# Projecting q, k and v of the second token half transposed, with the rotary exchange by way of DRAM

## The chip, the cores and the metric

The kernel runs on one core of one Trainium2 chip. The metric is the device time of one execution in microseconds (us).

## The reference

One decoder layer over 1024 tokens of width 1024, in float32. The change concerns the softmax attention of the first sub-layer. Of the combined input projection, 512 columns are q (8 heads of 64), 128 are k and 128 are v (2 heads of 64 each):

```python
proj = h @ w_in[l]
aq, ak, av, hq, hf, hi, hg = jnp.split(proj, _SPLITS, axis=-1)
aq = partial_rope(aq.reshape(B, T, ATT_Q_HEADS, ATT_HEAD_DIM))
ak = partial_rope(ak.reshape(B, T, ATT_KV_HEADS, ATT_HEAD_DIM))
...
attn = sliding_window_sink_attention(aq, ak, av, attn_sinks[l])   # window 128, blocks of 128
attn = rmsnorm(attn, attn_out_w[l])
```

`partial_rope` rotates only the first 16 of the 64 dimensions of a head: with x1 and x2 the first and second 8 of them, it gives x1·cos − x2·sin and x2·cos + x1·sin, where the angle depends on the token. The attention output and that of a gated linear recurrence (from hq, hf, hi, hg) go through one output projection; a dense MLP with hidden width 4096 follows.

## The kernel before

The sequence is cut into 8 blocks of 128 tokens (tb 0 to 7) in two halves (0 to 3, 4 to 7). The normed input h is held transposed (model dimension on the partitions, tokens along the row), for each of 8 slices of the model dimension and each half, as a high and a low part (`hhi`, `hlo`); weights are split likewise. `proj3` forms a product as three matmuls per slice, so one projection of 8 slices is 24 matmuls.

Natural layout: for each block, `hhi`/`hlo` of the block are the stationary operand and the weights stream, giving q as 128 tokens by 512 columns (`pq`) and k with v as 128 by 256 (`pk`). ScalarE (ACT) moves these to SBUF (`q`, `kv`), and `rope` rotates in place along the row, on GpSimd (POOL) for most blocks. The projections of the first half are done in an earlier, hand-ordered stage; those of blocks 4 and 5 of q run while the second half's h is being finished.

`attention(tb)` is a generator with three parts. Part one turns q (four transposes to `pqT`, one ACT copy to `qT`) and k (one transpose to `pkT`, one VectorE (DVE) copy to `kT`), forms the scores `sc` against the block itself and the block before it, copies them into `comb` (ACT copies the previous block's half, DVE's masked copies, COPY_PREDICATED, the block's own), takes the row maximum (`mx`), the exponentials (eight on ACT, into `comb`, with sums), and divides. Part two turns the probabilities (`pT`), masks them into `pc` and `pp`, multiplies with v into `oT`, and starts the norm: `sqa`, `sqr`, a transpose `ssp`, `ssc`, two small POOL operations ending in `r_att`, and `dg`. Part three is the matmul `rb` and a multiplication of `q`. A loop of 16 steps calls these parts for block tb at steps tb+4, tb+6 and tb+7, and after them `filler(i)`: for i below 8 the q or the k/v projection of a second-half block with its rope, above that `values(i-8)`, the projection `pv` of the recurrence's values (24 matmuls of 128x512, from weights `whv`). Instructions are not pinned in this stretch: a scheduler chooses the order on each engine, and each engine then runs its list in that order, waiting at whatever is not ready. Loads are issued from the SyncE (SP) queue; `wada` and `whv` in the rows below are weight loads. After the loop come the recurrence's head projections (`phf`, `phq`, `phg`).

All operations are recorded by a helper, so every row of the profile reads L39.

Of the kernel before, what the change touches and what calls it, by code (L numbers as in the profile page):

```python
# [47 lines left out]
def hybrid_layer(ctx: ExitStack, tc: tile.TileContext, I, out, dbg=None):  # L48
# [476 lines left out]
    def htok(tb):  # L525
        sl = slice(tb % 4 * P, tb % 4 * P + P)
        return [(hh[k][tb // 4][0][:, sl], hh[k][tb // 4][1][:, sl]) for k in range(KB) if hh[k][tb // 4]]
# [2 lines left out]
        return [hh[k][th] for k in range(KB)]  # L530

    qn, kvn = [], []
    cosT = cload("cosT", [P, TB, 16], pool=XA)
    sinT = cload("sinT", [P, TB, 16], pool=XA)

    def qproj(tb):
        if tb < 6:
            pq = pq0[tb]
        else:
            pq = mm_ps(f"pq{tb}")  # L540
            proj3(pq, htok(tb), wq)
        q = m_(f"q{tb}")
        ACT.activation(q, pq, AF.Copy, scale=0.125)
        qn.append(q)

    def kvproj(tb):
        if tb < 4:
            pk = pk0[tb]
        else:
            pk = mm_ps(f"pk{tb}")  # L550
            proj3(pk[:, :256], htok(tb), wkv)
        kv = XA.tile([P, 256], F32, tag="kv", bufs=8, name=f"kv{tb}")
        ACT.activation(kv, pk[:, :256], AF.Copy)
        kvn.append(kv)

    def rope(tb, nh, eng=POOL):
        base = qn[tb] if nh == 8 else kvn[tb][:, 0:P]
        v3 = base.rearrange("p (h d) -> p h d", d=64)
        rt = t_(f"rt{tb}_{nh}", (P, 2, 8, 16))
        t1, t2 = rt[:, 0], rt[:, 1]  # L560
        cb = cosT[:, tb:tb + 1, :].broadcast_to([P, nh, 16])
        s0 = sinT[:, tb:tb + 1, 0:8].broadcast_to([P, nh, 8])
        s1 = sinT[:, tb:tb + 1, 8:16].broadcast_to([P, nh, 8])
        eng.tensor_tensor(t1[:, :nh, :], v3[:, :, 0:16], cb, ALU.mult)
        eng.tensor_tensor(t2[:, :nh, 0:8], v3[:, :, 8:16], s0, ALU.mult)
        eng.tensor_tensor(t2[:, :nh, 8:16], v3[:, :, 0:8], s1, ALU.mult)
        eng.tensor_tensor(v3[:, :, 0:16], t1[:, :nh, :], t2[:, :nh, :], ALU.add)


    sinks = cload("sinks", [P, 8], pool=tiny1)  # L570
# [1 line left out]
    mle = cload("mle", [P, P], I32, pool=XA)  # L572
    fle = cload("fle", [P, P], pool=XA)
    attT = [None] * TB
    kTs, vs = {}, {}

    def attention(tb):
        q, kv = qn[tb], kvn[tb]
        pqT = tp_ps(f"pqT{tb}")
        for m in range(4):  # L580
            PE.transpose(pqT[:, m * P:(m + 1) * P], q[:, m * P:(m + 1) * P], ident)
        qT = t_(f"qT{tb}", [P, 4, P])
        ACT.activation(qT, pqT.rearrange("p (m t) -> p m t", m=4), AF.Copy)
        pkT = tp_ps(f"pkT{tb}")
        PE.transpose(pkT[:, :P], kv[:, 0:P], ident)
        kT = XA.tile([P, P], F32, tag="kT", bufs=3, name=f"kT{tb}")
        DVE.tensor_copy(kT, pkT[:, :P])
        kTs[tb] = kT
        aw = q
        a3 = aw.rearrange("p (m t) -> p m t", m=4)  # L590
        c5 = w_(f"comb{tb}", (P, 2, 2, 2, P))
# [49 lines left out]
                DVE.tensor_tensor(pp[:, mp], pT3, pc[:, mp], ALU.subtract)  # L641
        o_ps = tp_ps(f"oT{tb}")
        for g in range(2):
            vsl = slice(128 + 64 * g, 192 + 64 * g)
            og = o_ps[64 * g:64 * g + 64, :].rearrange("p (a x) -> p a x", a=2)
            if tb:
                PE.matmul(og, lhsT=kvn[tb - 1][:, vsl],
                          rhs=pp[:, :, 2 * g:2 * g + 2, :].rearrange("p a m q -> p a (m q)"), start=True, stop=False)
            PE.matmul(og, lhsT=kv[:, vsl], rhs=pc[:, :, 2 * g:2 * g + 2, :].rearrange("p a m q -> p a (m q)"),
                      start=(tb == 0), stop=True)  # L650
        sq = t_(f"sqa{tb}")
        ACT.activation(sq, o_ps, AF.Square)
# [19 lines left out]
            next(att[tb])  # L672

    att = [attention(tb) for tb in range(TB)]
    pq0.append(a_ps("pq4"))
    for kb in range(KB):
        if 0 < kb < KB - 1:
            if kb + 2 < KB:
                DVE.tensor_tensor(xT1[kb + 2], xT1[kb + 2], rbx, ALU.mult)
            first_evac(1, kb + 1, xT1[kb + 1])  # L680
        (qproj if kb < 4 else kvproj)(kb % 4)
        if kb == 0:
            pq0.append(mm_ps("pq5"))
        for tb in (4, 5):
            proj3(pq0[tb], htok(tb)[kb:kb + 1], wq[kb:kb + 1], kb == 0, kb == KB - 1)
    for tb in range(4):
        eng = DVE if tb < 2 else POOL
        rope(tb, 8, eng)
        rope(tb, 2, eng)
    pin(False, ACT, DVE, POOL, PE)  # L690

    def filler(i):
        if i < 8:
            (kvproj if i % 2 else qproj)(4 + i // 2)
            rope(4 + i // 2, 2 if i % 2 else 8)
        else:
            values(i - 8)


    whv = []  # L700
    hv = []
# [1033 lines left out]
def layout(x, c, w_ada, b_ada, pre_w_mix, w_in, attn_sinks, attn_out_w, lb_table,  # L1735
           hg_norm_w, w_out, post_w_mix, pre_w_mlp, w_up, w_down, post_w_mlp):
    A = {}
    f = lambda a: np.ascontiguousarray(a)
    cols = lambda v: f(np.asarray(v).reshape(-1, P).T)
    A["x"] = f(np.asarray(x)[0])  # L1740
    A["xT1"] = f(np.asarray(x)[0, 512:].T.reshape(KB, P, 512))
    t_cT = cols(np.asarray(c)[0])
    wa = np.asarray(w_ada)[0]
    w1 = wa[:, :2048]
    A["wada1"] = f(w1.reshape(4, 2, P, 2, 4, 256).transpose(3, 4, 0, 2, 1, 5).reshape(2, 4, 4, P, 512))
    A["wada1"][:, 2:] = (w1.reshape(2, 4, P, 2, 4, 256)[:, :, :, :, 2:].transpose(0, 4, 1, 2, 3, 5)
                         .reshape(2, 2, 4, P, 512))
# [32 lines left out]
    A["cosT"] = f(np.concatenate([co, co], 1).reshape(TB, P, 16).transpose(1, 0, 2))  # L1780
    A["sinT"] = f(np.concatenate([-si, si], 1).reshape(TB, P, 16).transpose(1, 0, 2))
# [21 lines left out]
```

## Time and profile before

| | |
|---|---|
| median of 3 runs (lowest to highest) | 1086.75 us (1086.56 to 1087.96) |
| the profiled execution | 1086.42 us, of it span 1084.6 us |
| mean granted TensorE (PE) clock | 0.998 |
| busy: PE, DVE, ACT, POOL | 1067.8, 798.8, 587.6, 371.3 us |
| DMA | 205.74 MB, mean 190 GB/s |

Rows of the profile give first the times (start and duration in us, or the sum and the mean), then the engine, the operation, and the written tile, an arrow and the tiles read. A group written "x24" is so many instructions in a row. Busy shares are means over stages that have different limits; what this change touches lies between about 60 and 220 us of the span.

### The profile page before, as it was taken

The numbers are of one execution on the slowest core, as the hardware profiler recorded it, in microseconds if no ns is written. First come the engines' busy times: TensorE is split into PE (matmuls) and PEld (weight loads), VectorE is DVE, ScalarE is ACT, GpSimd is POOL, SyncE is SP. The second block draws the span as 40 slices with busy tenths as digits, with TensorE's granted clock in tenths as the row PEclk, the third lists the DMA queues.
The fourth block names the chain that finished last, engine by engine and source line by source line (L and its number), as shares of the span: only waits on it lengthen the run. The fifth ranks groups of instructions, "written<-read, shape, count | busy, mean of one in ns | idle before, by whom it ended". The sixth has DMA issues, their size and how long they took to land.

```text
span 1084.6 us, 16059 instructions
## 1 busy us (share of the span) xinstructions
PE 1067.8 (98%) x5449; PEld 872.2 (80%) x5449; DVE 798.8 (74%) x1331; ACT 587.6 (54%) x1213; POOL 371.3 (34%) x497
## 2 busy tenths in 40 slices
PE   8999999999999999999999999999999999999996
PEld 6887676788888888888888888888888888888885
DVE  4877778878865664558776757776777787899886
ACT  4556443446456655575655555555665543556434
POOL 1263211233335653423444435334323333300014
PEclk9999999999999999999999999999999999999999
DMA  9903102444211252323676777767998888988638
GB/s 361 342 21 122 35 1 80 155 141 142 80 59 55 88 179 88 131 94 127 213 255 236 258 251 233 256 207 254 318 374 290 263 288 273 322 304 276 184 96 139
DMA packets 102979, 205.74 MB, mean 190 GB/s; under 512 B 13168, under 2 KB 13936, under 8 KB 102896
## 3 DMA queue, kind: packets, MB, share of 16 engines
q1 hardware_dynamic: 87408, 157.14, 42.9%
q0 software_dynamic: 15200, 47.20, 14.4%
q8 instruction: 43, 0.70, 0.3%
q10 hardware_dynamic: 288, 0.36, 0.1%
q14 instruction: 40, 0.33, 0.1%
HBM read 149.60 MB, written 55.05 MB: 189 GB/s over the span
## 4 chain that ended last, share of the span: by engine, by line
PE 89%; DVE 4%; DMA 4%; ACT 1%; issue 1%; POOL 1%; SPq 0%; DVEq 0%; ACTq 0%; POOLq 0%
PE pda L39 16%; PE pua L39 14%; PE pdc L39 8%; PE po L39 8%; PE puc L39 7%; PE pu L39 4%; PE pdb L39 4%; PE phg L39 4%; PE pub L39 4%; PE phf L39 3%; PE pv L39 3%; PE phq L39 3%; PE pq L39 3%; DMA wa<-wada 2%; PE o L39 1%; PE pk L39 1%
## 5 line engine op out<-in xcount | busy, mean ns | idle before, releaser
L39 POOL TENSOR_TENSOR b<-b,b 128x512 f32<-128x512 f32 x64 | 87.4, 1365 | 223.4 <-DMA b<-w_dn 223.0
L39 ACT ACTIVATE s<-s 128x512 f32<-128x512 f32 x84 | 53.0, 630 | 32.4 <-DVE s L39 31.0
L39 ACT ACTIVATE dw<-dwr 128x512 fp32r<-128x512 f32 x72 | 45.4, 630 | 43.1 <-DMA dwr<-td 24.9
L39 DVE TENSOR_TENSOR dw<-dwr,dw 128x512 fp32r<-128x512 f32 x72 | 55.6, 772 | 6.6 <-ACT dw L39 6.6
L39 DVE TENSOR_TENSOR acc<-pda,acc 128x512 f32<-128x512 f32 x68 | 47.1, 693 | 15.9 <-PE pda L39 15.5
L39 POOL DMA_DIRECT2D td<-b x64 | 36.3, 567 | 19.0 <-POOL b L39 19.0
L39 POOL TENSOR_TENSOR rrf<-ssf,mhalf 128x1 f32<-128x1 f32 x7 | 7.7, 1103 | 98.4 <-DVE ssf L39 98.4
L39 ACT ACTIVATE s<-pua 128x512 f32<-128x512 f32 x28 | 16.7, 597 | 41.4 <-PE pua L39 35.9
L39 DVE TENSOR_TENSOR wt<-s,wt 128x512 fp32r<-128x512 f32 x42 | 36.1, 859 | 2.6 <-ACT wt L39 2.5
L39 ACT ACT_TABLE_LOAD x28 | 35.9, 1283 | 1.7 <-PEq L1796 1.2
L39 DVE SCALAR_TENSOR_TENSOR macc<-wada,cs,macc 128x512 f32<-128x512 f32 x42 | 33.7, 802 | 2.4 <-DMA wada<-wada 1.8
L39 POOL DMA_DIRECT2D b<-w_dn x64 | 34.4, 540 | 2.5 <-issue 2.5
L39 DVE TENSOR_TENSOR wt<-a,wt 128x512 fp32r<-128x512 f32 x42 | 34.5, 823 | 0.9 <-ACT wt L39 0.9
L39 PE MATMUL pua<-bt_1h,wt 128*128 128x512 f32 x84 | 32.7, 389 | 0.0
L39 PE MATMUL pua<-bt_3h,wt 128*128 128x512 f32 x84 | 32.7, 389 | 0.0
L39 PE MATMUL pua<-bt_0h,wt 128*128 128x512 f32 x84 | 32.7, 389 | 0.0
L39 PE MATMUL pua<-bt_2h,wt 128*128 128x512 f32 x84 | 32.7, 389 | 0.0
L39 DVE TENSOR_TENSOR s<-puc,s 128x512 f32<-128x512 f32 x14 | 9.7, 691 | 31.0 <-issue 28.6
L39 POOL TENSOR_TENSOR comb<-comb,rd 128x512 f32<-128x512 f32 x8 | 11.7, 1458 | 59.9 <-DVE rd L39 44.2
L39 ACT ACTIVATE wt<-s 128x512 fp32r<-128x512 f32 x42 | 26.3, 626 | 6.9 <-DVE s L39 6.7
L39 PE MATMUL pda<-dw,du_7h 128*128 128x512 f32 x96 | 29.6, 389 | 0.0
L39 PE MATMUL pdc<-dw,du_3h 128*128 128x512 f32 x96 | 29.6, 389 | 0.0
(768 smaller groups left out, 3750.6 us busy)
## 6 DMA issues: line engine op xcount, KB each, us to landing
dur<-ud SPq DMA_DIRECT2D x112, 256.0 KB, 4.5
wada<-wada SPq DMA_DIRECT2D x64, 256.0 KB, 3.3
b<-w_dn POOLq DMA_DIRECT2D x64, 256.0 KB, 5.1
td<-b POOLq DMA_DIRECT2D x64, 256.0 KB, 3.2
dwr<-td SPq DMA_DIRECT2D x64, 256.0 KB, 4.0
a<-w_u SPq DMA_DIRECT2D x56, 256.0 KB, 3.9
dwr<-w_dn SPq DMA_DIRECT2D x48, 256.0 KB, 4.5
ud<-s SPq DMA_DIRECT2D x42, 256.0 KB, 3.3
```

The costliest lines, as they stand in the source:

```text
L39: ins = op(*args, **kw)
```

## The change

For blocks 4 to 7, the roles of the matmul operands are swapped: slices of the weights (128 columns) become stationary and the half's h (512 tokens) streams. q comes out as four tiles `pqT1_0` to `pqT1_3` of 128 dimensions by 512 tokens, k as `pkT1`, v as `pvT1`, each from 24 matmuls of 128x512. q and k are then already in the layout that the scores need: the transposes `pqT` and `pkT` of blocks 4 to 7, and the copies after them, go. v needs natural layout and is turned by four transposes with an ACT copy on each side (`v_turn`).

The rotary dimensions now lie on partitions, where the two members of a pair can't be brought together within a row. So the weight columns are permuted until the rotary dimensions of a pair of heads sit on partitions 48 to 79 (the host tables for the first half follow suit), and these rows are written to a DRAM buffer (`ropeq`, eight DMAs; `ropek`, four), read back twice, once in order (`ropeq1`) and once with the 8-row groups exchanged (`ropeq2`), rotated by three DVE operations, and returned to `q` or `kT1` by four DMAs each. The 32 POOL operations (24 rows of its list) of the second half's ropes go with that. All of these DMAs are issued from SP.

```diff
+    kT1 = XA.tile([P, 512], F32, tag="kT1", name="kT1")
+    v1 = XA.tile([P, 512], F32, tag="v1", name="v1")
+    def half_mm(pst, w, ks=range(KB)):
+        ks = list(ks)
+        proj3(pst, [w[k] for k in ks], [hh[k][1] for k in ks], ks[0] == 0, ks[-1] == KB - 1)
+    def q_evac(m):
...
+        for j in range(4):
+            ACT.activation(qn[4 + j][:, m * P:(m + 1) * P], pq1[m][:, j * P:(j + 1) * P], AF.Copy, scale=0.125)
+    ropeq = dram.tile([8, 4, 8, 512], F32, tag="ropeq", name="ropeq")
+    ropek = dram.tile([8, 4, 8, P], F32, tag="ropek", name="ropek")
+    def rotate(R, Rr, n):
+        for t, tab in ((R, cosR), (Rr, sinR)):
+            t3 = t.rearrange("p (m x) -> p m x", m=n)
+            DVE.tensor_tensor(t3, t3, tab.unsqueeze(1).broadcast_to([P, n, P]), ALU.mult)
+        DVE.tensor_tensor(R, R, Rr, ALU.add)
+    def q_rope():
+        R, Rr = t_("ropeq1"), t_("ropeq2")
+        for w in range(2):
+            for j in range(4):
+                SP.dma_start(ropeq[2 * j:2 * j + 2, 2 * w:2 * w + 2], qn[4 + j][48:80, :])
+        for w, t in enumerate((R, Rr)):
+            SP.dma_start(t, ropeq[:, w:w + 2])
+        rotate(R, Rr, 4)
+        for j in range(4):
+            SP.dma_start(qn[4 + j][48:80, :], R[32 * j:32 * j + 32, :])
...
+    def v_turn(pst):
+        vT = t_("vT1")
+        ACT.activation(vT, pst, AF.Copy)
+        pvT = tp_ps("pvT1")
+        for j in range(4):
+            PE.transpose(pvT[:, j * P:(j + 1) * P], vT[:, j * P:(j + 1) * P], ident)
+        ACT.activation(v1, pvT, AF.Copy)
...
+        else:
+            qT = q.rearrange("p (m t) -> p m t", m=4)
+            kTs[tb] = kT1[:, (tb - 4) * P:(tb - 3) * P]
...
     def filler(i):
-        if i < 8:
-            (kvproj if i % 2 else qproj)(4 + i // 2)
-            rope(4 + i // 2, 2 if i % 2 else 8)
-        else:
+        if i == 0:
+            q_evac(0)
+            q_evac(1)
+        elif i == 1:
+            pq1.append(mm_ps("pqT1_2"))
+            half_mm(pq1[2], wqc[2], lo_k)
...
+        elif i == 4:
+            pq1.append(mm_ps("pqT1_3"))
+            half_mm(pq1[3], wqc[3])
+            q_evac(3)
+            q_rope()
+        elif i == 5:
+            pq1.append(mm_ps("pkT1"))
+            half_mm(pq1[4], wcols(wkv, 0), lo_k)
...
+        elif i > 7:
             values(i - 8)
```

The scheduler moves instructions in consequence. Three places matter below. The number behind a tile's name only counts tiles; rows are in the order in which the engine runs them.

First, PE where the scores of block 1 (`sc1`) begin. Before, `pk6` is the k/v projection of block 6:

```order
L39 MATMUL pk6_1210<-wkv1h_452,hlo3_1_858 128x256
L39 MATMUL pk6_1210<-wkv2h_575,hhi4_1_872 128x256
L39 MATMUL pk6_1210<-wkv2l_576,hhi4_1_872 128x256
L39 MATMUL pk6_1210<-wkv2h_575,hlo4_1_873 128x256
L39 MATMUL sc1_0_0_1157<-kT0_1068,qT1_1150 128x128
L39 MATMUL sc1_0_1_1158<-kT0_1068,qT1_1150 128x128
```

After the change:

```order
L39 MATMUL pvT1_1333<-hhi7_1_924,wkv3h_678 128x512
L39 MATMUL pvT1_1333<-hlo7_1_925,wkv3h_678 128x512
L39 MATMUL pvT1_1333<-hhi7_1_924,wkv3l_679 128x512
L39 MATMUL pv0_1611<-whv0h_1563,hhi0_0_307 128x512
L39 MATMUL sc1_0_0_1144<-kT0_1039,qT1_1137 128x128
L39 MATMUL sc1_0_1_1145<-kT0_1039,qT1_1137 128x128
```

Before, `sc1` stands behind 72 rows of 128x512 (`pq4`, `pq5`, `pq6`) and 63 of 128x256 (`pk4`, `pk5`, 15 of `pk6`) of the second half's projections; now it stands behind all 144 of 128x512 and one of `pv0`.

Second, PE in a steady step, where the norm's transpose `ssp2`, the scores of block 4 and the matmul `rb2` stand. Before:

```order
L39 MATMUL pv1_1789<-whv4l_1635,hhi4_0_596 128x512
L39 MATMUL ssp2_1535<-c_tab_97,sqr2_1533 128x128
L39 MATMUL pv1_1789<-whv4h_1634,hlo4_0_597 128x512
L39 MATMUL sc4_0_0_1557<-kT4_1554,qT4_1550 128x128
L39 MATMUL sc4_0_1_1558<-kT4_1554,qT4_1550 128x128
L39 MATMUL sc4_0_0_1557<-kT3_1418,qT4_1550 128x128
```

and, after ten more rows of `sc4`,

```order
L39 MATMUL sc4_1_1_1572<-kT4_1554,qT4_1550 128x128
L39 MATMUL rb2_1685<-dg2_1543,ones_99 128x128
L39 MATMUL pT3_0_1690<-c_tab_97,comb3_1420 128x128 x4
L39 MATMUL pT3_1_1697<-c_tab_97,comb3_1420 128x128 x4
L39 MATMUL pv1_1789<-whv5h_1640,hhi5_0_640 128x512
```

After the change:

```order
L39 MATMUL sc4_1_0_1524<-kT1_827,q4_989 128x128
L39 MATMUL ssp2_1499<-c_tab_97,sqr2_1497 128x128
L39 MATMUL sc4_1_1_1525<-kT1_827,q4_989 128x128
L39 MATMUL sc4_1_0_1524<-kT3_1394,q4_989 128x128
L39 MATMUL sc4_1_1_1525<-kT3_1394,q4_989 128x128
L39 MATMUL sc4_1_0_1524<-kT1_827,q4_989 128x128
L39 MATMUL sc4_1_1_1525<-kT1_827,q4_989 128x128
L39 MATMUL pT3_0_1643<-c_tab_97,comb3_1396 128x128
L39 MATMUL rb2_1638<-dg2_1507,ones_99 128x128
L39 MATMUL pT3_0_1643<-c_tab_97,comb3_1396 128x128 x3
L39 MATMUL pT3_1_1650<-c_tab_97,comb3_1396 128x128 x4
L39 MATMUL pv2_1851<-whv7h_1605,hhi7_0_774 128x512
```

Of the three `pv` that stood around `ssp2`, and the others of a step, 21 are left between one `oT` and the next where there were 26; fewer rows separate `ssp2` from `rb2`.

Third, DVE where the masked copies of block 1's scores into `comb1` stand. Before:

```order
L39 COPY kT1_1154<-pkT1_1152 128x128
L39 TENSOR_TENSOR den0_1107<-sm0_1098,es0_1096 128x8
L39 RECIPROCAL rd0_1109<-den0_1107 128x8
L39 TENSOR_TENSOR comb0_1070<-comb0_1070,rd0_1109 128x512
L39 COPY_PREDICATED comb1_1156<-c_mle_827,sc1_0_0_1157 128x256
L39 COPY_PREDICATED comb1_1156<-c_mle_827,sc1_0_1_1158 128x256
L39 COPY_PREDICATED comb1_1156<-c_mle_827,sc1_1_0_1171 128x256
L39 COPY_PREDICATED comb1_1156<-c_mle_827,sc1_1_1_1172 128x256
L39 TENSOR_REDUCE mx1_1185<-comb1_1156 128x8
```

After the change:

```order
L39 TENSOR_TENSOR comb0_1041<-comb0_1041,rd0_1080 128x512
L39 TENSOR_TENSOR whv4l_1588<-whv4r0_1589,whv4h_1587 128x512
L39 TENSOR_TENSOR whv5l_1594<-whv5r0_1595,whv5h_1593 128x512
L39 TENSOR_TENSOR whv6l_1600<-whv6r0_1601,whv6h_1599 128x512
L39 TENSOR_TENSOR ropeq1_1113<-ropeq1_1113,c_cosR_823 128x512
L39 TENSOR_TENSOR ropeq2_1114<-ropeq2_1114,c_sinR_825 128x512
L39 COPY_PREDICATED comb1_1143<-c_mle_835,sc1_0_0_1144 128x256
L39 TENSOR_TENSOR ropeq1_1113<-ropeq1_1113,ropeq2_1114 128x512
L39 COPY_PREDICATED comb1_1143<-c_mle_835,sc1_0_1_1145 128x256
L39 COPY_PREDICATED comb1_1143<-c_mle_835,sc1_1_0_1158 128x256
L39 COPY_PREDICATED comb1_1143<-c_mle_835,sc1_1_1_1159 128x256
L39 TENSOR_TENSOR pc0_1210<-pT0_0_1211,c_fle_837 128x512
```

The multiplications of `ropeq1` and `ropeq2`, which need the DRAM round trip, now stand ahead of all four masked copies, and the addition behind the first.

The round trip on SP is new there; before, the loads `whv3r` to `whv7r` are followed at once by `wada2_0_0`:

```order
L39 DMA whv5r0_1642<-w_hv 128x512
L39 DMA whv6r0_1648<-w_hv 128x512
L39 DMA whv7r0_1654<-w_hv 128x512
L39 DMA wada2_0_0_2146<-wada 128x512
L39 DMA wada2_0_1_2149<-wada 128x512
L39 DMA wada2_0_2_2152<-wada 128x512
```

After the change:

```order
L39 DMA whv6r0_1601<-w_hv 128x512
L39 DMA ropeq_829<-q4_989 2x16x512
L39 DMA ropeq_829<-q5_990 2x16x512
L39 DMA ropeq_829<-q6_991 2x16x512
L39 DMA ropeq_829<-q7_992 2x16x512
L39 DMA ropeq_829<-q4_989 2x16x512
L39 DMA ropeq_829<-q5_990 2x16x512
L39 DMA ropeq_829<-q6_991 2x16x512
L39 DMA ropeq_829<-q7_992 2x16x512
L39 DMA ropeq1_1113<-ropeq_829 128x1x512
L39 DMA ropek_830<-kT1_827 16x4x128 x2
L39 DMA ropeq2_1114<-ropeq_829 128x1x512
```

The eight writes, the first read, two of k's writes and the second read now stand between `whv6r` and `whv7r`.

More of the change, by code (lines that the diff above doesn't have):

```diff
@@ L532, in hybrid_layer @@
     qn, kvn = [], []
[L533 to L541 removed]
+    kTs, vs = {}, {}
+    cosT = cload("cosT", [P, 4, 32], pool=XA)
+    sinT = cload("sinT", [P, 4, 32], pool=XA)
+    cosR = cload("cosR", [P, P], pool=XA)
+    sinR = cload("sinR", [P, P], pool=XA)
+    def qproj(tb):
         q = m_(f"q{tb}")
[L543 removed]
+        ACT.activation(q, pq0[tb], AF.Copy, scale=0.125)
@@ L544, in qproj @@
         qn.append(q)
     def kvproj(tb):
[L547 to L553, printed above, removed]
-        kvn.append(kv)
+        kv = XA.tile([P, 256], F32, tag="kv", bufs=4, name=f"kv{tb}")
+        ACT.activation(kv, pk0[tb][:, :256], AF.Copy)
+        kvn.append(kv)
+        vs[tb] = [kv[:, 128 + 64 * g:192 + 64 * g] for g in range(2)]
@@ new lines, in wcols @@
+    def wcols(w, c):
+        return [(hi[:, c:c + P], lo[:, c:c + P]) for hi, lo in w]
+    kT1 = XA.tile([P, 512], F32, tag="kT1", name="kT1")
+    v1 = XA.tile([P, 512], F32, tag="v1", name="v1")
+    pq1 = []
+    def half_mm(pst, w, ks=range(KB)):
+        ks = list(ks)
+        proj3(pst, [w[k] for k in ks], [hh[k][1] for k in ks], ks[0] == 0, ks[-1] == KB - 1)
+    def q_evac(m):
+        if not m:
+            qn.extend(m_(f"q{tb}") for tb in range(4, TB))
+        for j in range(4):
+            ACT.activation(qn[4 + j][:, m * P:(m + 1) * P], pq1[m][:, j * P:(j + 1) * P], AF.Copy, scale=0.125)
@@ new lines, in k_rope @@
+    def k_rope():
+        Rk = t_("ropek", (P, 2, P))
+        R, Rr = Rk[:, 0], Rk[:, 1]
+        for w in range(2):
+            for g in range(2):
+                dst = ropek.rearrange("(t g) s e x -> g s e t x", g=2)[g, 2 * w:2 * w + 2]
+                SP.dma_start(dst, kT1[48 + 16 * g:64 + 16 * g, :])
+        for w, t in enumerate((R, Rr)):
+            SP.dma_start(t, ropek[:, w:w + 2])
+        rotate(R, Rr, 1)
+        for j in range(4):
+            SP.dma_start(kT1[48:80, j * P:(j + 1) * P], R[32 * j:32 * j + 32, :])
@@ new lines, in rope @@
+        rt = t_(f"rt{tb}_{nh}", (P, 2, 4, 32))
+        t1, t2 = rt[:, 0, :n], rt[:, 1, :n]
+        eng.tensor_tensor(t1, v3, cosT[:, tb:tb + 1, :].broadcast_to([P, n, 32]), ALU.mult)
+        v4, t4 = (t.rearrange("p m (g d) -> p m g d", g=2) for t in (v3, t2))
+        s4 = sinT[:, tb, :].rearrange("p (g d) -> p g d", g=2).unsqueeze(1).broadcast_to([P, n, 2, 16])
+        for b in range(2):
+            bs, cs_ = slice(8 * b, 8 * b + 8), slice(8 - 8 * b, 16 - 8 * b)
+            eng.tensor_tensor(t4[:, :, :, bs], v4[:, :, :, cs_], s4[:, :, :, bs], ALU.mult)
@@ L570, in hybrid_layer @@
+        eng.tensor_tensor(v3, t1, t2, ALU.add)
     sinks = cload("sinks", [P, 8], pool=tiny1)
@@ L574, in hybrid_layer @@
     attT = [None] * TB
-    kTs, vs = {}, {}
     def attention(tb):
[L578 to L588, printed above, removed]
+        q = qn[tb]
+        if tb < 4:
+            pqT = tp_ps(f"pqT{tb}")
+            for m in range(4):
+                PE.transpose(pqT[:, m * P:(m + 1) * P], q[:, m * P:(m + 1) * P], ident)
+            qT = t_(f"qT{tb}", [P, 4, P])
+            ACT.activation(qT, pqT.rearrange("p (m t) -> p m t", m=4), AF.Copy)
+            pkT = tp_ps(f"pkT{tb}")
+            PE.transpose(pkT[:, :P], kvn[tb][:, 0:P], ident)
+            kT = XA.tile([P, P], F32, tag="kT", bufs=3, name=f"kT{tb}")
+            DVE.tensor_copy(kT, pkT[:, :P])
+            kTs[tb] = kT
+        else:
+            qT = q.rearrange("p (m t) -> p m t", m=4)
+            kTs[tb] = kT1[:, (tb - 4) * P:(tb - 3) * P]
+            vs[tb] = [v1[:, (tb - 4) * P + 64 * g:(tb - 4) * P + 64 * g + 64] for g in range(2)]
         aw = q
@@ L674, in hybrid_layer @@
     att = [attention(tb) for tb in range(TB)]
-    pq0.append(a_ps("pq4"))
+    wqc = [wcols(wq, m * P) for m in range(4)]
+    pq1.append(a_ps("pqT1_0"))
     for kb in range(KB):
@@ L682, in hybrid_layer @@
         if kb == 0:
-            pq0.append(mm_ps("pq5"))
-        for tb in (4, 5):
-            proj3(pq0[tb], htok(tb)[kb:kb + 1], wq[kb:kb + 1], kb == 0, kb == KB - 1)
+            pq1.append(mm_ps("pqT1_1"))
+        for m in range(2):
+            half_mm(pq1[m], wqc[m], (kb,))
     for tb in range(4):
@@ L690, in hybrid_layer @@
     pin(False, ACT, DVE, POOL, PE)
+    lo_k, hi_k = range(4), range(4, KB)
     def filler(i):
-        if i < 8:
-            (kvproj if i % 2 else qproj)(4 + i // 2)
-            rope(4 + i // 2, 2 if i % 2 else 8)
-        else:
+        if i == 0:
[4 more added lines that the diff above has]
+            half_mm(pq1[2], wqc[2], lo_k)
+        elif i == 3:
+            half_mm(pq1[2], wqc[2], hi_k)
+            q_evac(2)
+        elif i == 4:
[6 more added lines that the diff above has]
+            half_mm(pq1[4], wcols(wkv, 0), lo_k)
+        elif i == 6:
+            half_mm(pq1[4], wcols(wkv, 0), hi_k)
+            ACT.activation(kT1, pq1[4], AF.Copy)
+            k_rope()
+            pq1.append(mm_ps("pvT1"))
+            half_mm(pq1[5], wcols(wkv, P), lo_k)
+        elif i == 7:
+            half_mm(pq1[5], wcols(wkv, P), hi_k)
+            v_turn(pq1[5])
+        elif i > 7:
             values(i - 8)
```

32 lines of the change are left out of this document (15 added, 17 removed).

## The prediction

> **What bounds the kernel now.** I read the page first: busy shares and the chain that ended last.
>
> ```profile
> PE 1067.8 (98%) x5449; PEld 872.2 (80%) x5449; DVE 798.8 (74%) x1331; ACT 587.6 (54%) x1213; POOL 371.3 (34%) x497
> PE 89%; DVE 4%; DMA 4%; ACT 1%; issue 1%; POOL 1%; SPq 0%; DVEq 0%; ACTq 0%; POOLq 0%
> ```
>
> PE is the bound over the whole span; work taken off PE shortens the kernel if PE doesn't wait for it elsewhere. So the next view is what PE waits for:
>
> ```profile
> PE rb L39 <- DVE dg L39: 1.6, 4, 0.6
> PE ssp L39 <- DVE sqr L39: 0.7, 2, 0.4
> PE phg L39 <- ACT f L39: 0.5, 1, 0.5
> ```
>
> (Total, times, longest.) The first two lie in the attention and are small; after 200 us PE waits for `phg` once and then nearly never. So PE's lateness at `phg`, beyond that half microsecond, is the kernel's lateness: nothing behind it gives time back.
>
> That PE hardly waits doesn't say that the attention has room. The chain of waits from 97 us, in order of time:
>
> ```profile
> 104.22 3.09 ACT comb L39 x16
> ...
> 112.69 0.49 PE rb L39 x2
> 113.17 0.87 PE pT L39 x8
> 114.05 4.79 PE pv L39 x21
> 118.84 1.87 PE oT L39 x8
> ...
> 131.43 1.87 PE oT L39 x8
> 133.30 0.58 PE pqT L39 x4
> 133.89 0.11 PE pkT L39
> ```
>
> Up to 112.69 the chain runs through ACT and DVE, from there through PE. One `oT` follows another by 131.43 − 118.84 = 12.59 us. DVE in the same step, with its idle time in brackets:
>
> ```profile
> 120.46 0.17 DVE L39 TENSOR_TENSOR den<-sm,es 128x8 f32<-128x8 f32 x1 [2.16 <-ACT comb L39]
> ...
> 122.11 1.06 DVE L39 TENSOR_REDUCE sqr<-sqa 128x128 f32<-128x512 f32 x1
> 123.08 0.29 DVE L39 COPY kT<-pkT 128x128 f32<-128x128 f32 x1
> 123.59 0.29 DVE L39 TENSOR_REDUCE ssc<-ssp 128x1 f32<-128x128 f32 x1 [0.23 <-PE ssp L39]
> 124.83 0.29 DVE L39 TENSOR_SCALAR dg<-c_tab,r_att 128x128 f32<-128x128 f32 x1 [0.94 <-POOL r_att L39]
> 125.11 1.45 DVE L39 COPY_PREDICATED comb<-c_mle,sc 128x256 f32<-128x256 int32 x4
> 126.44 0.68 DVE L39 TENSOR_TENSOR q<-q,rb 128x512 f32<-128x512 f32 x1
> 127.04 1.21 DVE L39 TENSOR_REDUCE mx<-comb 128x8 f32<-128x1024 f32 x1
> ...
> 129.51 0.17 DVE L39 TENSOR_TENSOR sd<-c_sinks,mx 128x8 f32<-128x8 f32 x1
> ```
>
> and ACT's exponentials:
>
> ```profile
> 90.49 0.39 ACT L39 ACTIVATE comb<-comb,nm 128x128 f32<-128x128 f32 x1
> ...
> 129.70 0.40 ACT L39 ACTIVATE comb<-comb,nm 128x128 f32<-128x128 f32 x1 [0.36 <-DVE sd L39]
> ...
> 132.80 0.19 ACT L39 ACTIVATION_READ_ACCUMULATOR comb<-comb,nm 128x1 f32 x1
> ...
> 167.40 0.40 ACT L39 ACTIVATE comb<-comb,nm 128x128 f32<-128x128 f32 x1 [1.80 <-DVE sd L39]
> ```
>
> This is a loop: `den` waits for the exponentials (2.16 us), DVE then works almost without a gap to `sd` at 129.51, and `sd` releases the next exponentials. 9.2 us on DVE and 3.3 on ACT make 12.5, the step that PE also takes. Two bounds of nearly the same length run beside each other; shortening PE's alone leaves the other.
>
> **PE's work.** The second half's projections and `sc1`:
>
> ```profile
> 59.93 9.08 PE pq L39 x40
> 69.01 5.75 PE pk L39 x48
> ...
> 84.38 2.06 PE L39 MATMUL sc<-kT,qT 64*128 64x128 f32 x32
> ```
>
> A 128x512 matmul costs 9.08/40 = 0.227 us, a 128x256 one 5.75/48 = 0.120. q keeps its 96 of 512. k and v go from 96 × 0.120 = 11.5 to 48 × 0.227 = 10.9: −0.6. The transposes of four blocks go, 4 × (0.58 + 0.11) = −2.8, and v's four come, +0.6. PE's work: −2.8 us.
>
> Costed at nothing: the copies `qT` and `kT` that go (ACT isn't in the way; `kT` counts in the loop below), the sixteen smaller copies of q (ACT has idle time before `sc1`), the 32 rope operations on POOL that go (the POOL of the loop is `r_att`, which waits for `ssc`), and v's turn, whose result is first needed by `oT4`, some 50 us later. k's round trip has the same cover; what it holds up on SP are `whv7r` and `wada` loads, which are late by the same few us as their users.
>
> **The attention starts late.** `sc1` stands behind other work now. By the order, 72 × 0.227 + 63 × 0.120 = 23.9 us of the second half's projections preceded it, and 145 × 0.227 = 32.9 do now: 9.0 us later, at 84.4 + 9.0 = 93.4. From `sc1` to the exponentials took 90.49 − 84.38 = 6.1; the addition of the rope between the masked copies adds one 128x512 DVE operation (`q<-q,rb` above, 0.6 until the next begins). So the exponentials of block 1 start at 100.1, 9.6 late, if the round trip is in time.
>
> **What is caught up.** From there the DVE/ACT loop sets the pace, since PE has moved 24 or more matmuls out of the steps: between one `oT` and the next it has 21 `pv` instead of 26 and no transposes, 12.59 − 5 × 0.227 − 0.69 = 10.8 us of work. The loop loses the `kT` copy (0.2) and a little of the 0.94 wait for POOL, since two masked copies now fill it, but these delay `ssc` too: together −0.4, so 12.2. The six loops to block 7's exponentials took 167.40 − 90.49 = 76.9 and take about 74: 2.9 is caught up, 6.7 is left. PE finds 1.4 us per step of nothing to do, at `ssp` and `rb`.
>
> **The end of the stretch.** PE has the end of the attention and then the head projections.
>
> ```profile
> 185.01 1.87 PE oT L39 x8
> ...
> 188.48 1.39 PE phf L39 x6
> ...
> 217.28 5.76 PE phg L39 x24
> ```
>
> By the order 13 rows of `phf` preceded the last `rb` and 27 of `phf` and `phq` do now: 14 × 0.23 = 3.2 of the 6.7 is used. The late DVE delays the split of `whq0l` for the `phq` matmuls: I put 1.1 on it, between 0 and the 3 that DVE is still late. So +4.6, 1086.4 + 4.6 = 1091.0 by the execution shown. A second way gives the same: six steps from block 1 to 7, of which five or six wait 1.4, are 7 to 8.4 of waiting, less 2.8 of work.
>
> **The round trip.** DVE multiplies `ropeq1` and `ropeq2` ahead of block 1's masked copies, so the copies wait for writes, reads and landing. The trace has no write of this shape. Nearest rows:
>
> ```profile
> q1 hardware_dynamic: 87408, 157.14, 42.9%
> ud<-rl SPq DMA_DIRECT2D x6, 256.0 KB, 2.0
> whv5r<-w_hv SPq DMA_DIRECT2D x1, 256.0 KB, 2.6
> ```
>
> A packet (157.14 MB/87408 = 1.8 KB, one row of these tiles) holds an engine 0.429 × 16 × 1084.6/87408 = 0.085 us. The last part of q is copied out by about 85 (its matmuls end with `pqT1_3`, before `sc1`'s 24 + 24 of k and v); the eight writes are issued from 84.7 to 88.2. The cheap end: a write's 32 rows spread over 16 engines, two packets each; writes and reads land after 2.0 to 2.6, the second read waits for k's writes on SP, and `ropeq2` lands at about 94, within the 95 at which the first scores of `sc1` are there: nothing is added. The dear end: all 32 rows on one engine, 8 × 32 × 0.085 = 21.8; `ropeq2` lands at 84.7 + 2.0 + 21.8 + 2.6 = 111, +16. Between: the write's pattern is 2x16x512 in the order, and all the DMAs timed above are 128 rows outermost. If its two outermost entries are what is divided, two engines get 16 rows each, 8 × 16 × 0.085 = 10.9: the writes end at 97.6, the read lands at 100.2, with its multiplication 100.8 to 101.2, where the copies would have begun at 95: +6.2, which moves the whole loop and isn't caught up. I take this, since no row shows a pattern with a narrow outermost dimension spreading, and keep both ends.
>
> The Trainium skill, in "DMA: Bandwidth & Descriptors", section "Why a DMA increments its semaphore by 16 and not by 1", states that a DMA uses as many of the 16 engines as the largest number that divides the outermost dimension of both patterns, so 2 for these writes. By it the sum would be 1097; if the writes spread, 1091. No run here shows it yet.
>
> Sum: −2.8 of work, +7.4 of waiting, +6.2 of round trip = +10.8, 1086.42 + 10.8 = 1097.2. The median of the runs shown is 0.33 above the profiled execution: 1097.5.
>
> **The rivals.** One: the writes spread, the round trip is hidden, and only the late start costs: 1091.0 + 0.3 ≈ 1091.4 (1089 to 1094, by 11.9 to 12.4 for a loop). For it speaks the row of `ud<-rl`: 256 KB written and landed 2.0 us after the issue, four times the bytes of one of these writes.
>
> Two, on the other side: the loop isn't 12.2 but as short as PE's 10.8, because the waits on PE (`ssp`, 0.23) and POOL (0.94) and on ACT's other copies shrink when PE is free earlier. Then 6 × (12.8 − 10.8) = 12 are made up, more than the 9.6 lost, PE never waits and the work sets the end: 1086.4 − 2.8 + 0.3 ≈ 1084. It decides where the waiting on PE from `sc1` to the last `rb` sums to less than 2.8. Against it: DVE's idle in the step apart from the exponentials is only 1.2.
>
> Three: the two cancel; the loop is about 11.5, waiting 2 to 5 us: 1084.6 to 1088.9, within 0.2%, or 2.2 us, which is about what a measurement of this kernel can tell from no change.
>
> Four: the round trip is dearer than two engines make it, or k's return holds up `sc4` as well: 1101 to 1110.
>
> **How the numbers follow.** Round trip on the path as forecast (1094 to 1100.5): 0.48. Late start only: 0.26. Cancelled: 0.11. Work alone: 0.10. Dearer: 0.05. The first two hold 0.74; with most of the third, from 1087, 0.8. So 1087 to 1100.5; faster 0.10, same 0.11, slower 0.79.
>
> **What would show it.** `sc1` starting near 93.4 and not 84.4; DVE's `ropeq2` multiplication near 100.5 with 4 us or more of idle before it put down to a DMA (rival one: about 95, idle under 1); block 1's exponentials at 106 (100 in rival one, 97 or less in two); `oT` to `oT` 12.2 with waits of about 1.4 at `ssp` and `rb`; PE's busy sum in the stretch about 3 us down and its waits for `dg` and `sqr` up from 2.3 to 7 or more; `phg` at about 228 against 217.28. I'm wrong if `ropeq2` is in time, if the loop shrinks with PE's work, or if PE's lateness at `phg` isn't that of the end.

## The result, and the profile after

| | median | lowest to highest | ratio to before (95% interval) |
|---|---|---|---|
| before | 1086.7 us | 1086.3 to 1088.0 | |
| the change | 1104.7 us | 1102.5 to 1105.5 | 1.016 (1.0149 to 1.0171) |

18 us slower, where 10.8 were forecast. The profiled execution took 1105.5, of it span 1103.7. The page, busy shares and the chain that ended last:

```profile
PE 1073.1 (97%) x5385; PEld 874.5 (79%) x5385; DVE 803.0 (73%) x1333; ACT 586.2 (53%) x1220; POOL 365.3 (33%) x465
PE 84%; DVE 6%; DMA 5%; ACT 3%; issue 1%; POOL 1%; SPq 0%; DVEq 0%; POOLq 0%; ACTq 0%
```

PE has 64 matmuls less and is busy 5.3 us more: some of them ran slowly. Its idle time, the span less the busy time, grew from 16.8 to 30.6 us, by 13.8; the two make the 19.1 by which the span grew. What PE waits for (total, times, longest):

```profile
PE pT L39 <- DVE comb L39: 8.6, 2, 8.0
PE ssp L39 <- DVE sqr L39: 3.9, 5, 1.0
PE rb L39 <- DVE dg L39: 3.8, 7, 0.6
```

The second and third are the waits of before, grown from 2.3 to 7.7; the first is new. DVE behind block 0, where the masked copies of block 1 (`comb`) now queue, and SP:

```profile
87.71 0.68 DVE L39 TENSOR_TENSOR whv6l<-whv6r,whv6h 128x512 fp32r<-128x512 f32 x1
99.46 0.69 DVE L39 TENSOR_TENSOR ropeq<-ropeq,c_cosR 128x512 f32<-128x512 f32 x1 [11.07 <-DMA ropeq<-ropeq]
103.08 0.69 DVE L39 TENSOR_TENSOR ropeq<-ropeq,c_sinR 128x512 f32<-128x512 f32 x1 [2.93 <-DMA ropeq<-ropeq]
103.69 0.43 DVE L39 COPY_PREDICATED comb<-c_mle,sc 128x256 f32<-128x256 int32 x1
```

```profile
84.76 5.28 SPq L39 DMA_DIRECT2D ropeq<-q  x8
92.25 0.64 SPq L39 DMA_DIRECT2D ropeq<-ropeq  x1
98.26 0.63 SPq L39 DMA_DIRECT2D ropeq<-ropeq  x1
```

DVE stands still for 11.07 and 2.93 us. On SP a read is issued when its writes have landed: the first four at 92.25, the other four at 98.26. The scores were ready: PE ran `sc1` at 93.6, as worked out (93.4), and then stood for 8.0 us. ACT's exponentials of blocks 1 and 7 (`es` stands beside them; it was at 90.38 and 167.80):

```profile
109.22 0.19 ACT L39 ACTIVATE es<-sd 128x8 f32<-128x8 f32 x1
...
188.96 0.20 ACT L39 ACTIVATE es<-sd 128x8 f32<-128x8 f32 x1
```

Block 1 is 18.8 late and block 7 is 21.2 late: nothing was caught up, six steps took 79.7 against 77.4. PE between 151 and 163 us shows why (columns: length, busy time of PE, PEld, DVE, ACT and POOL with instructions, then PE's granted clock, DMA share, GB/s):

```profile
151.00:155.00 4.00, 2.48 (x27) 1.85 (x26) 3.00 (x7) 1.34 (x5) 1.30 (x3) 1.00 0.00 0
155.00:159.00 4.00, 4.00 (x16) 3.44 (x17) 4.00 (x10) 0.00 (x0) 0.00 (x0) 0.57 0.00 0
159.00:163.00 4.00, 4.00 (x20) 2.85 (x20) 0.89 (x3) 3.77 (x18) 0.00 (x0) 1.00 0.00 0
```

First PE is idle for 1.5 of 4 us in short pieces, then busy throughout at a clock of 0.57, then at 1.00 again. The chain of waits shows the price, the 21 `pv` of a step without and with a lowered clock:

```profile
143.67 4.80 PE pv L39 x21
148.47 1.93 PE oT L39 x8
...
156.57 5.92 PE pv L39 x21
162.49 1.93 PE oT L39 x8
```

The second `phg`, whose lateness is the kernel's, started at 217.28 before; now it is 19.1 late, as is the span:

```profile
236.36 3.71 PE phg L39 x15
```

### The profile page after: what moved, and what is told of

It reads as the page before. It is cut to its first block, busy times and chain, and to the rows that moved or that the text cites. A ratio compares the mean times of both kernels' runs of the same rounds, so it can differ in the third digit from the quotient of the medians.

```text
span 1103.7 us, 15952 instructions
## 1 busy us (share of the span) xinstructions
PE 1073.1 (97%) x5385; PEld 874.5 (79%) x5385; DVE 803.0 (73%) x1333; ACT 586.2 (53%) x1220; POOL 365.3 (33%) x465
## 4 chain that ended last, share of the span: by engine, by line
PE 84%; DVE 6%; DMA 5%; ACT 3%; issue 1%; POOL 1%; SPq 0%; DVEq 0%; POOLq 0%; ACTq 0%
PE pda L39 16%; PE pua L39 14%; PE pdc L39 8%; PE po L39 8%; PE puc L39 7%; PE pu L39 4%; PE pdb L39 4%; PE phg L39 3%; PE phf L39 3%; PE pub L39 3%; PE phq L39 3%; PE pv L39 2%; DMA wa<-wada 2%; PE pqT L39 1%; ACT comb L39 1%; PE o L39 1%
## 5 line engine op out<-in xcount | busy, mean ns | idle before, releaser
L39 POOL TENSOR_TENSOR b<-b,b 128x512 f32<-128x512 f32 x64 | 90.7, 1417 | 222.3 <-DMA b<-w_dn 222.0
L39 DVE TENSOR_TENSOR dw<-dwr,dw 128x512 fp32r<-128x512 f32 x72 | 51.6, 717 | 5.5 <-ACT dw L39 5.5
L39 ACT ACTIVATE comb<-comb,nm 128x128 f32<-128x128 f32 x64 | 24.8, 388 | 13.7 <-DVE nm L39 7.7
L39 DVE TENSOR_TENSOR acc<-pdc,acc 128x512 f32<-128x512 f32 x36 | 24.6, 684 | 9.3 <-PE pdc L39 9.2
```

The costliest lines, as they stand in the source:

```text
L39: ins = op(*args, **kw)
```

## The experiments

The theory from this profile: DVE's wait for the round trip, long through the narrow writes; then a late start; then PE's short waits, which lower its clock. The rivals are in the expectations.

**Wide writes.**

```diff
-                SP.dma_start(ropeq[2 * j:2 * j + 2, 2 * w:2 * w + 2], qn[4 + j][48:80, :])
+                for t, eng in enumerate((SP, POOL)):
+                    eng.dma_start(ropeq[2 * j + t, 2 * w:2 * w + 2], qn[4 + j][48 + 16 * t:64 + 16 * t, :])
```

> The eight writes of q's rotary rows become sixteen, each of 16 rows of 512 outermost instead of 2x16x512, eight issued from SP and eight from GpSimd; same bytes, and the order of PE and DVE is that of the changed kernel. Theory (the writes are slow because their outermost dimension of 2 puts them on two engines): all writes land by about 93, DVE's multiplication of ropeq2 starts at 96 to 98 instead of 103.1, the kernel takes 1104.7 - 6 = about 1098.5. If in addition the lower clock of 150 to 190 us comes from the one long wait of PE at 96 to 104, the clock stays at 1 and the time is about 1093. Rival (the round trip is long through its number of steps and the latency to DRAM, whatever the shape): the multiplication stays near 103, 1104 or more.

1098.0 us, 1.011 (1.0093 to 1.0127). SP and DVE:

```profile
90.11 0.75 SPq L39 DMA_DIRECT2D ropeq<-ropeq  x1
92.14 0.61 SPq L39 DMA_DIRECT2D ropeq<-ropeq  x1
```

```profile
97.76 0.69 DVE L39 TENSOR_TENSOR ropeq<-ropeq,c_sinR 128x512 f32<-128x512 f32 x1 [2.42 <-DMA ropeq<-ropeq]
```

The writes are done 6 us earlier, and the multiplication starts 5.3 earlier, as the theory has it. The clock still fell, to 0.85 between 150 and 160 us, without an 8 us wait of PE ahead of it (PE's longest wait was 2.4). But the queues changed along with the shape; so a cleaner run:

**Flat writes:** only the destination's pattern differs. This kernel leaves out the order of the rows that the rotation needs.

```diff
-                SP.dma_start(ropeq[2 * j:2 * j + 2, 2 * w:2 * w + 2], qn[4 + j][48:80, :])
+                r0 = 32 * (4 * w + j)
+                SP.dma_start(ropeq.rearrange("b s e x -> (b s e) x")[r0:r0 + 32], qn[4 + j][48:80, :])
```

> The changed kernel with one thing different in the eight writes of q's rotary rows: each goes to 32 rows of the DRAM buffer that lie one after another (32x512) instead of two groups of 16 (2x16x512). Same queue, same number, same bytes; the rows that come back are then not those that the rotation needs, and the first read waits for all eight writes. Theory (the outermost dimension of 2 puts a narrow write on two engines): the last write lands about 2 after its issue, near 91, the reads are issued there and not at 92 and 98, DVE multiplies ropeq2 at 95 to 97 instead of 103.1, and the time is 1096 to 1099, as with sixteen wide writes from two queues. Rival (writes of rows to DRAM from one queue are slow whatever their shape): the last one lands near 98 again, 1103 or more.

1099.4 us, 1.0114 (1.0097 to 1.0131): 5.3 less than the change, and 0.4 above what the theory gave. SP, and the DMA view (KB each, median us from issue to landing):

```profile
84.74 4.25 SPq L39 DMA_DIRECT2D ropeq<-q  x8
...
90.66 1.44 SPq L39 DMA_DIRECT2D ropeq<-ropeq  x2
```

```profile
ropeq<-q SPq DMA_DIRECT2D x8, 64.0 KB, 1.7
```

```profile
97.55 0.69 DVE L39 TENSOR_TENSOR ropeq<-ropeq,c_sinR 128x512 f32<-128x512 f32 x1 [1.67 <-DMA ropeq<-ropeq]
```

All eight have landed by 90.66, where the last four narrow ones were done at 98.26: a write of the same bytes from the same queue lands in 1.7 us with 32 rows outermost. In the change, with 2 outermost, the last one took 8.75 from its issue at 89.43:

```profile
89.43 8.75 DMA ropeq<-q
```

While the writes are under way, the DMA share (the last number but one) of the change is 0.13, two of the 16 engines, and that of the flat run, in the second line, 0.49:

```profile
88.00:90.00 2.00, 2.00 (x11) 1.65 (x10) 0.39 (x1) 1.09 (x2) 0.00 (x0) 1.00 0.13 50
```

```profile
88.00:90.00 2.00, 2.00 (x11) 1.65 (x10) 0.37 (x1) 1.09 (x2) 0.00 (x0) 1.00 0.49 132
```

That the shape of the write is the cause is shown. Each of the two reads still took 4.5 to 6 us. They have 8 rows outermost in DRAM, and the loads of `whv7` and `wada` come right behind them (the DMA share of the flat run is 0.93 to 1.03 from 94 to 98 us); which of the two makes them slow wasn't tried.

**No round trip:** `q_rope()` and `k_rope()` are left out.

> The rotary rotation of the second half is left out altogether: no writes, reads or multiplications of ropeq and ropek. The scheduler then puts only 12 of pkT1 ahead of sc1, so the attention starts about as early as in the kernel before. Theory (all of the loss comes from the round trip and the order that goes with it): PE's saved work remains, 1084 to 1087. Rival (the transposed projections cost by themselves, since the steps are left with too little for PE): 1092 or more.

1094.35 us, 1.0067 (1.0052 to 1.0082). The rival's time: 7.6 of the 18 remain without any round trip, and with the exponentials of block 1 at 93.8, only 3.4 late. PE's waits:

```profile
PE ssp L39 <- DVE sqr L39: 4.3, 6, 1.1
PE rb L39 <- DVE dg L39: 4.0, 7, 0.6
```

**No round trip, late start:** the matmuls of `pkT1` and `pvT1` are issued before `sc1`, with an order between them.

```diff
+            half_mm(pq1[4], wcols(wkv, 0))
...
+            mark["pv"] = half_mm(pq1[5], wcols(wkv, P))
...
+        if tb == 1:
+            PE.last = mark["pv"].ins
```

> The rotary rotation of the second half is left out, and all 24 matmuls each of pkT1 and pvT1 are forced ahead of sc1, so that PE's order is nearly that of the changed kernel from sc1 on. This is the late start without the round trip. By the terms of the prediction: sc1 near 94, exponentials of block 1 near 100, 1091.4. If PE's short waits in each step lower its clock without the long wait before, the clock falls below 1 between 150 and 190 us too and the time is 1093 to 1097. If the late start costs nothing: 1085.

1094.03 us, 1.0068 (1.0053 to 1.0083): equal to the run before it within their spread (1092.9 to 1096.2, and 1092.5 to 1095.6), though the exponentials of block 1 start at 100.55 instead of 93.8. **Between these two the late start costs nothing**; with steps in which PE doesn't wait it wasn't tried. What the two have in common is the waiting, 8.1 and 8.3 us at `ssp` and `rb`. The clock fell here too, as the expectation's second case has it, after the same pattern, with no long wait anywhere:

```profile
142.00:146.00 4.00, 2.48 (x27) 1.85 (x24) 3.05 (x8) 1.32 (x4) 1.25 (x3) 0.94 0.00 0
146.00:149.00 3.00, 3.00 (x12) 2.81 (x13) 2.80 (x6) 0.00 (x0) 0.00 (x0) 0.51 0.00 0
```

**Filled waits.**

```diff
+        for _ in range(6 if 1 < tb < 7 else 0):
+            PE.matmul(ssp[:, P:], lhsT=ones_r, rhs=hh[0][0][0][:, P:], start=True, stop=True)
...
+            for _ in range(5):
+                PE.matmul(ssp[:, P:], lhsT=ones_r, rhs=hh[0][0][0][:, P:], start=True, stop=True)
```

> The changed kernel with eleven added matmuls of 128x384 in each of the steps of blocks 2 to 6, six before and five after the transpose ssp, into an unused part of its tile: about 1.9 us of needless PE work per step, where PE waited. Theory (the waits lower the clock, and the lower clock lengthens the steps): the granted clock stays at 1.00 from 120 to 190 us, the steps of 13.4 to 14.7 us shrink to about 12.5, and the kernel gets faster by 3 to 5 in spite of the added work, about 1100.5. Rival (the long wait before, or something else, lowers the clock, or the steps are bound by DVE and ACT alone): the clock dips as before and the time is 1104 to 1108.

1108.0 us, 1.0198 (1.0183 to 1.0213). The time is the rival's, the clock is the theory's:

```profile
155.00:159.00 4.00, 3.29 (x35) 2.69 (x32) 1.76 (x6) 1.32 (x4) 0.74 (x2) 1.00 0.00 0
159.00:163.00 4.00, 4.00 (x22) 3.41 (x21) 4.00 (x10) 0.83 (x2) 0.00 (x0) 1.00 0.00 0
```

With PE idle for 0.7 instead of 1.5 of 4 us, and the same 8 us wait before, the clock stayed at 1.00 in every step: the short waits of the step are what lowers it. But the added work takes as much as the clock gave back: the last four steps are 13.3 each (mean of the change 13.6), and fewer of the head projections' matmuls stand ahead of the last `rb`. Needless work is no cure.

**Rotation later:** DVE's three operations on `ropeq` behind the masked copies of block 2.

```diff
+        keep, DVE.last = DVE.last, mark["cp"].ins
         rotate(R, Rr, 4)
+        DVE.last = keep
```

> The changed kernel with its writes as they are (2x16x512), but DVE's three operations on ropeq1 and ropeq2 are ordered behind the masked copies of block 2's scores instead of ahead of block 1's. Nobody then waits for the round trip; sc1 still stands behind all of pkT1 and pvT1, and PE's steps have 21 pv and nothing of them between oT and rb. Theory (the round trip cost what DVE waited for it, 11 to 14 us, of which block 1's exponentials were 8 late): the exponentials of block 1 start near 100.5, and the time is that of the kernel without the rotation, 1093 to 1096. Rival (the wait moves to another place, because the rows return late to q or k): above 1099.

1103.5 us, 1.0153 (1.014 to 1.0167): the rival's time, but not for its reason. `comb1`'s copies ran at 95.5, but the wait moved within the same queues:

```profile
104.16 0.69 DVE L39 TENSOR_TENSOR whv7l<-whv7r,whv7h 128x512 fp32r<-128x512 f32 x1 [4.61 <-ACT whv7h L39]
```

`whv7`'s load stands on SP behind the reads, which wait for the writes, and DVE waits for its split. Costing the held-up load "late as its user" was wrong: DVE has it ahead of work that others wait for.

**Steps written out:** PE's order of blocks 2 to 6 pinned as it stood before, and 18 `pv` put ahead of block 2's step.

```diff
+            step(t - 1)          # rb
+            next(att[t])         # pT
+            some(21)             # pv
+            next(att[t])         # oT
+            some(3)
+            next(att[t + 2])     # four sc
+            some(1)
+            step(t)              # ssp
+            some(1)
+            step(t + 2)          # twelve sc
```

Without the rotation:

> The rotation of the second half is left out, as in the run without the rotation (1094.35), and PE's order in the steps of blocks 2 to 6 is written out by hand as it stood before: after oT three pv, four sc, one pv, ssp, one pv, twelve sc, rb, the eight pT, 21 pv; 26 pv in a step instead of 21. Theory (the loss that remains without a round trip is PE waiting at ssp and rb, because the new order leaves only sc between oT and rb): PE's waits at ssp and rb fall from 8.3 to under 3, the clock stays at 1.00, 1084.5 to 1087. Rival (the step is bound by DVE and ACT, and PE's waiting only moves to oT or pT): 1091 or more.

1091.3 us, 1.0035 (1.0023 to 1.0047): 3.0 of the 7.6 are gone. One wait of 3.1 us was new, at `ssp6`, where only four `pv` stood ahead, and the clock fell behind it. With that step mended too:

> The rotation of the second half is left out, and the steps of blocks 2 to 5 are written out as in the first run of that kind; in addition the step of block 6 is written out as it stood before the change: after oT nine pv, the eight pT of block 7, one pv, ssp, and pv up to rb. The earlier run left four pv and nothing else ahead of ssp6, where PE waited 3.1 us and the clock fell to 0.80 to 0.86 behind it. Theory (PE's waits at ssp and rb are the loss that is left without a round trip): ssp6's wait falls under 0.5, the clock stays at 1.00, 1085 to 1088. Rival (the transposed form's steps are bound otherwise): 1090 to 1092, as the earlier run.

1087.6 us, 1.0009 (1.0000 to 1.0018), as the theory has it. The windows from 100 to 210 us all have a clock of 1.00, and what PE waits for is

```profile
PE ssp L39 <- DVE sqr L39: 3.1, 6, 0.6
PE rb L39 <- DVE dg L39: 0.3, 1, 0.3
```

So the order in the steps cost 1094.35 − 1087.6 = 6.8. Yet the 2.8 us of saved work don't show: the exponentials are 12.6 apart in this run as before the change. The chain of waits from one block's exponentials to the next is

```profile
131.31 0.50 ACT comb L39 x2
...
134.63 0.18 DVE den L39
...
143.82 0.08 DVE sd L39
143.92 0.49 ACT comb L39 x2
```

with nothing of PE in it but `ssp` (0.32). That is the loop of the prediction: 3.3 us on ACT and 9.2 from `den` to `sd`, as long as before. Less work on PE doesn't shorten it; PE waits up to 0.6 in each step for it. PE's busy sum, too, is only 0.4 below that of before (1067.4 to 1067.8); where the rest of the 2.8 went wasn't taken apart.

**The whole computation with cures.** Wide writes, rotation later, the steps in their first written-out form (with the wait of some 3 us at `ssp6`); then the same with narrow writes:

> The whole computation: the transposed projections with the sixteen wide writes (16 rows outermost, half of them from GpSimd), the rotation behind the masked copies of block 2, 12 matmuls of pkT1 ahead of sc1, and the written-out steps with 26 pv. Theory: as the run without rotation and with these steps, plus at most 1 for the three DVE operations: 1085 to 1088, so equal to the kernel before or up to 1.5 faster. Rival (the steps are bound by DVE and ACT): 1092 or more.

1101.8 us, 1.0141 (1.0127 to 1.0155), the rival's time.

> As the run with all three cures (wide writes, rotation late, written-out steps), but with the eight narrow writes of the change, 2x16x512 from SP. Theory (the shape of the writes costs only what somebody waits for): ropeq2's multiplication waits little or not at all, and the time is within 1.5 of the run with wide writes. Rival (the narrow writes hold up other transfers on the same engines, the whv and wada loads): 3 or more slower.

1107.8 us, 1.0189 (1.0175 to 1.0203), the rival: 6.0 slower than with wide writes. Both fail as the run with the later rotation did, at `whv7`, for which DVE waited here before block 1's copies, 7.34 us with wide and 12.27 with narrow writes:

```profile
95.76 0.69 DVE L39 TENSOR_TENSOR whv7l<-whv7r,whv7h 128x512 fp32r<-128x512 f32 x1 [7.34 <-ACT whv7h L39]
```

```profile
100.62 0.69 DVE L39 TENSOR_TENSOR whv7l<-whv7r,whv7h 128x512 fp32r<-128x512 f32 x1 [12.27 <-ACT whv7h L39]
```

Its load, too, took longer to land beside the narrow writes, 7.03 us and not 4.39 (first the run with wide writes), as the rival has it:

```profile
90.68 4.39 DMA whv7r<-w_hv
```

```profile
92.91 7.03 DMA whv7r<-w_hv
```

Then nothing that others need stands behind the round trip: `whv7` from GpSimd's queue and behind block 1's scores, the rotation on GpSimd behind `r_att`.

```diff
+                if kb == 7:
+                    ACT.last, DVE.last = mark["ac1"].ins, mark["cp1"].ins
+                whv.append(load_split(g_, f"whv{kb}", I["w_hv"][kb], raw=load_raw(
+                    raw_, f"whv{kb}r0", I["w_hv"][kb], POOL) if kb == 7 else None))
...
+        keep, POOL.last = POOL.last, rmark[0].ins
+        rotate(R, Rr, 4, POOL)
```

> The whole computation, with the round trip out of everybody's way: sixteen wide writes from SP and GpSimd, whv7's load issued from GpSimd's queue (it stood behind the round trip on SP) and its split on ACT and DVE behind the scores of block 1, the rotation of q and k on GpSimd, each at a place where its rows have landed, 12 matmuls of pkT1 ahead of sc1, and the written-out steps. PE's and DVE's order is that of the run without the rotation. Theory (what queued behind the round trip, on DVE and on SP, was its whole cost): within 1.5 of that run, 1085 to 1089. Rival (the round trip costs by itself, by its 2 MB or by GpSimd's work): 1092 or more.

1092.3 us, 1.0045 (1.0032 to 1.0058), the rival by a little.

> As the whole computation with the round trip out of the way, but with the eight narrow writes (2x16x512 from SP) of the change. Theory (the shape of the writes costs what somebody waits for): the rows land near 103 instead of 95, GpSimd's rotation begins near 103 and ends near 108, before it has to divide block 2's probabilities near 110; the time is within 1.5 of the run with wide writes. Rival (the rows are too late for GpSimd, or the narrow writes hold up loads on the engines that they share): 3 or more slower.

1091.7 us, 1.0046 (1.0031 to 1.0060): with nobody waiting for them, narrow and wide writes are equal within the spread, as the theory has it. 13 us of the 18 are cured here, but no version with the whole computation beats the kernel before. The remaining 4.4 over the run without rotation weren't taken apart. Two rows of the run with wide writes bear on them: PE's wait for the turned q of blocks 1 and 2, and DVE's `dg`, which took 1.29 instead of 0.29 while GpSimd multiplied `ropeq` beside it.

```profile
PE sc L39 <- ACT qT L39: 2.5, 2, 2.0
```

```profile
102.26 1.29 DVE L39 TENSOR_SCALAR dg<-c_tab,r_att 128x128 f32<-128x128 f32 x1 [0.98 <-POOL r_att L39]
```

```profile
102.21 1.25 POOL L39 TENSOR_TENSOR ropeq<-ropeq,c_cosR 128x512 f32<-128x512 f32 x1
```

## Why the prediction was wrong in size, and where it was right

The prediction added three terms: −2.8 of PE's work, +7.4 of waiting in the steps, +6.2 for the round trip. The two pages allow the same sum. PE's idle time grew by 13.8, where 7.4 + 6.2 = 13.6 were forecast. PE's busy time was to fall by 2.8 and grew by 5.3. **The failed step is the term of PE's work.** It was costed at full speed, as if waiting cost only the time that PE waits; but the waits lowered PE's clock, and no term stands for that. These 8.1 are nearly all of the 8.3 between the forecast and the profiled execution. An estimate of the clock's part from the traces: four stretches of some 3.4 us with PE busy at half rate, one behind the 8 us wait and three in the steps, cost 1.7 each, 6.8 together. The rest is work that was not saved: in the run without the rotation, with one such stretch, PE was busy 1067.7, so that without it the busy time would have fallen by 1.8 and not by 2.8.

By medians of runs the 18.0 us come apart so, each part good to a microsecond or two: the shape of the writes 5.3 (1104.7 to 1099.4); the rest of the round trip 5.4 (to 1094.0, no round trip with PE's order nearly that of the change); PE's order in the steps, with the clock that it lowers, 6.4 (to 1087.6, where the attention also starts 6.9 earlier); 0.9 remains to the 1086.7 of before.

- *The writes.* Right, and for the reason given: the last was to land at 97.6 and did at 98.2, the forecast's value between two ends. The rule of the Trainium skill, "DMA: Bandwidth & Descriptors", section "Why a DMA increments its semaphore by 16 and not by 1", by which such a write goes to 2 engines, agrees with the DMA share of 0.13, two of 16; the writes were to take 1.36 each, and the last four took 6.0.
- *The reads.* Mis-sized: 2.6 from the row of a 128-row load, where the second read took 4.8 (98.26 to DVE's 103.08). With it the exponentials of block 1 came 2.5 later than the 106.3 that the terms gave, and PE's wait there was 8.0 and not 6.2. That the idle time came out as forecast is in part luck: the waits at `ssp` and `rb` grew by 5.4 and not by 7.4. (They came to 7.7, but the sum took the forecast waits whole, where 2.3 were there before.)
- *"The attention starts late."* Its start was right (93.6), its cost wrong in kind. With 6.7 us more or less of late start the time is the same (1094.0 and 1094.35); the seeming net of 9.6 − 2.9 − 3.2 + 1.1 was not a mechanism. The second way of the sum was one: waiting of 1.4 a step, 7 to 8.4 in all, was measured as 8.1 to 8.3 without the round trip and 7.7 with it.
- *"The loop sets the pace, 12.2."* Right in kind for the first steps and too short by little: with a clock of 1.00 three steps took 37.4 (109.22 to 146.61), 12.5 each, and 12.6 in the run with the order mended; the 0.4 that the loop was to lose stayed. (Six loops of 12.2 would be 73.2, and 76.9 less six times 0.4 is 74.5; the 74 stands between.) From 142 us on, the loop is no longer that of DVE and ACT alone. In the profile after, the step is then one chain through PE as well: `oT`, 4.4 us of ACT, DVE and GpSimd up to `rb`, the rest of `pT` and the 21 `pv`, then `oT`, 148.47 to 162.49. So a slower PE lengthens the step: the three steps with the lowered clock took 42.35, 4.9 more than the three before. Six took 79.7 instead of 74; these 5.7 and the 2.5 of the reads are the 8.3 seen from the steps.
- *PE's saved work* gave nothing even where the clock stayed at 1.00: when the waits were cured the time was that of before. The prediction's own sentence, that shortening PE's bound alone leaves the other, held.
- *Rival two* (the loop shrinks with PE's work) and *three* fell. *One* (the writes spread) was made true by hand and gave 1098 to 1099 instead of 1091.4: the reads still came late, and the steps waited and lowered the clock.

## What to carry to other kernels

When a transfer replaces engine work, look at what stands behind its consumers in each in-order queue, the loads on the issuing queue too: taking one waiter away only brings the next. Before moving work out of a loop of two nearly equal bounds, ask what will stand between its dependent steps: the five matmuls that a step had more before (26, not 21) are those that stood where PE now has to wait; their number and their place weren't tried apart. Count also what waiting does to the clock: here it made the work itself slower. And look at the pattern of a DMA, not at its bytes.

## What the runs showed of the hardware that was not expected

PE's granted clock fell to one half for some 3.4 us after stretches in which no single wait exceeded 0.9 us: 1.5 us of idle in 4, in two or three pieces, was enough in three of six steps of the profiled execution, and 0.7 in 4 wasn't in any. It isn't a sure sign: the step before these three was idle for 1.64 of 4 us, and the clock stayed at 1.00.

```profile
139.00:143.00 4.00, 2.36 (x21) 1.73 (x20) 3.06 (x9) 1.23 (x4) 1.35 (x3) 1.00 0.00 0
```

The Trainium skill, "TensorE: Matmul & The Clock Gate", Part 1, puts the half rate behind an idle window of about 3.4 us and mentions micro-idle as a second way to it; here the micro-idle way is what the trace shows. The spread goes with it: six runs of the change lie between 1102.5 and 1105.5 with clocks from 0.993 down to 0.989, those of the kernel before mostly within 1 us. Eight writes of 64 KB with 2 outermost entries were done 13.4 us after the first was issued (84.76 to 98.18), the same bytes with 32 after 5.9 at most (84.74 to 90.66).
